# Hybrid attention and RWKV block: the recurrence written in six parts a step, the first norm kept in DRAM, pools handed over while the preparation ends

## The chip, the cores and the metric

The kernel runs on one core of a Trainium2 chip. The metric is the device time of one execution in microseconds. TensorE is PE in the profile, VectorE DVE, ScalarE ACT, GpSimd POOL and SyncE SP; SP issues all of the kernel's DMAs.

## What is computed

One layer of a hybrid backbone on 2048 latent tokens and 256 context tokens of width 1024, float32:

```python
h  = modulate(rmsnorm(x, norm1_g), shift1, scale1)       # hc: the same of the context
q, k, v, rw, gl = jnp.split(h @ w_in, IN_SPLITS, axis=-1)
ya = latent_window_attention(rope(q), rope(k), v, kc, vc, sink)   # 128-token blocks, |i-j| <= 128, and all context keys
# RWKV-7, both directions d, 8 heads of 64; each latent scan starts from that direction's context state
sa = jnp.einsum('bhvk,bhk->bhv', S, -kk_t)
S  = S * w_t[:, :, None, :] + sa[..., None] * b_t[:, :, None, :] + v_t[..., None] * k_t[:, :, None, :]
y  = jnp.einsum('bhvk,bhk->bhv', S, r_t)
yr = rwkv_output(y_d0 + y_d1, ...)                       # group norm, bonus, low-rank gate
ga, gr = jnp.split(jax.nn.sigmoid(gl), 2, axis=-1)
x = x + gate1 * ((ga * (ya @ w_branch_attn) + gr * (yr @ w_branch_rwkv)) @ w_out)
x = x + gate2 * (jnp.square(jax.nn.relu(h2 @ w_mlp_up)) @ w_mlp_down)   # h2: second norm, modulated
out = rmsnorm(x, norm_f_g)
```

## The kernel before

Large products are made of three float32r matmuls each: both operands are split into a high part (a rounding copy on ScalarE) and a low part (a subtraction, here on GpSimd), and high x high, high x low and low x high are summed in PSUM (`gemm`, L215 to L217).

*First norm and input projection.* Tokens are taken in three thirds of two blocks each: (0,256) and (256,512), then (1280,384) and (768,512), then (1664,384) and (2048,256), as (first token, count). `norm_block` loads and normalises a block (L180), transposes it on TensorE into `tr` (L186), modulates it on VectorE into `hf` (L188) and splits `hf` into `hh` (ScalarE, L192) and `hl` (GpSimd, L193). There is one pair of buffers for a third, so a third is split only when the third before it has been projected. `project` goes through 36 groups of 128 weight columns: 20 for queries, keys, values and RWKV inputs, 16 for the merge gates. For the first 1024 latents the gate groups are left for later: their `hf` goes to DRAM (`h_d`), and 32 gates (16 groups for each half of 512 tokens) are made beside the recurrence (`gate`, tile `gt`; 24 matmuls each, the weights `gw_raw` split in `load_gw`, L829 and L830).

*Preparation.* After each third, `prepare` works off windows of 256 tokens (2, 4 and 3 of them): short convolution, decays (`zz_ps`), key norms (`nb_ps`), bonus (`bon_ps`), cumulated decays, on VectorE, ScalarE and GpSimd with small matmuls. It leaves keys, values and factors in DRAM (`ka_d`, `bk_d`, `rho_d`, `v_d`).

*Recurrence.* Each direction goes through 36 steps of 64 tokens; four steps are a window. For a window, `gram` makes the 64 x 64 products of its chunks (L517, after loading `kg` and `bkg`), and `inverse` inverts the unit triangular matrices: transposes and 31 substitution steps of two operations on VectorE (L528 to L549), then the off-diagonal part on TensorE (`yp`, `zp`, L557 and L569). `before` loads a step's operands, transposes them (`tb`, L606) and makes its masked products (`gb`, L613, masked at L616 and L617). `chain` is the dependent part of one step of one direction: products with the state (L624, evicted to `g`, L626), times the inverse (L629, evicted half by ScalarE at L630, half by VectorE at L631), the new state (L636 and L639, scaled by decay at L642), the outputs (L650 and L654). The loop takes direction 0, then direction 1, of each step and calls the two next parts of the next window's grams and inverse after each.

*Beside it.* After every second step `beside` emits a whole attention block (`attention`: 16 score tiles `sc` with their minima on VectorE, L754, then `sT`, the exponentials and `ops`), three parts of the later adaLN rows (`adp`, L117) and three gates, and from the twelfth call on the attention branch's product with its weights (`branch`, L881 to L883, also in tile `gt`). 

*What sets the order.* The program is written in this order, and a scheduler decides at build time, from the order of writing, the dependences, the pools' buffers and estimated durations, which instruction stands where in each engine's queue. At run time each engine works off its queue in that order and waits on semaphores. Pools that close give their memory to those that open later. Behind the recurrence follow the merge (L990 on) and the MLP (`fu`, `fd`), which the change leaves as they are.

## Time and profile before

| what | us |
|---|---|
| median of three runs | 4351.41 |
| lowest, highest | 4349.32, 4365.3 |
| the profiled execution | 4355.38 |
| its span, first to last instruction | 4353.6 |

The program's stages in the trace, by the starts of TensorE's instructions: projections and preparations up to 997.2 us (last projection matmul), first chain matmul at 1134.3, last one's outputs at about 2410, two attention blocks until 2489, branches until 2537, merge until about 2950, MLP until 4353. A busy TensorE is read together with its granted clock, as a part of full speed: matmul times are modelled and overlap each other, so the same number of matmuls is busy for longer at a lower clock.

### The profile page before, as it was taken

How to read it: one execution, taken by the hardware profiler on the slowest of the kernel's cores; microseconds unless marked ns; L12 is line 12 of the kernel's file. 1: busy time of each engine (PE TensorE's matmuls, PEld its weight loads, DVE VectorE, ACT ScalarE, POOL GpSimd, SP SyncE). 2: the span in 40 equal slices, each digit the busy share in tenths (PEclk: the TensorE clock that was granted, in tenths of full speed). 3: DMA queues.
4: the chain of work that ended last, by engine and by line, in shares of the span. 5: the costliest groups of instructions: out<-in, count | busy, mean ns of one | idle time of the engine just before them, and what ended most of it. 6: DMA issues, size and time to landing. Idle time of an engine off the chain costs nothing.

```text
span 4353.6 us, 67896 instructions
## 1 busy us (share of the span) xinstructions
PE 3976.6 (91%) x26788; PEld 3218.5 (74%) x26788; DVE 2233.9 (51%) x3918; ACT 1305.1 (30%) x2332; POOL 1344.6 (31%) x1120
## 2 busy tenths in 40 slices
PE   7989969894899999989989768998999999999999
PEld 5868868793677777767767646777888888888887
DVE  2264286687556646656674245434444436443434
ACT  3353444553322322223222213332222123212121
POOL 3353554542111111001000046523433233433332
PEclk8979989895999999889989779999999999999999
DMA  6555556665444543354453145452211113221111
GB/s 216 143 183 155 160 159 190 175 200 177 140 116 123 165 128 112 112 144 147 120 160 110 45 133 186 161 172 75 83 54 58 39 55 120 73 63 50 48 49 49
DMA packets 581874, 527.84 MB, mean 121 GB/s; under 512 B 118452, under 2 KB 492948, under 8 KB 580532
## 3 DMA queue, kind: packets, MB, share of 16 engines
q1 hardware_dynamic: 581556, 523.50, 39.9%
q8 instruction: 211, 3.46, 0.3%
q14 instruction: 107, 0.88, 0.1%
HBM read 383.19 MB, written 140.18 MB: 120 GB/s over the span
## 4 chain that ended last, share of the span: by engine, by line
PE 59%; DVE 9%; DMA 4%; issue 2%; POOL 2%; ACT 1%; SPq 1%; POOLq 0%; DVEq 0%; ACTq 0%
PE fd L1185 5%; PE fd L1184 5%; PE fd L1186 5%; PE fu L215 5%; PE fu L216 5%; PE fu L217 5%; PE gb L613 2%; PE ops L788 2%; DVE st L545 1%; PE sc L744 1%; DVE itmp L534 1%; PE mm L1099 1%; PE mm L1100 1%; PE mm L1101 1%; DVE tn L536 1%
## 5 line engine op out<-in xcount | busy, mean ns | idle before, releaser
L215 PE MATMUL acc<-hh,w_hi 128*128 128x384 f32 (+6 forms) x1304 | 460.1, 355 | 24.6 <-DVE st L227 8.7
L216 PE MATMUL acc<-hl,w_hi 128*128 128x384 f32 (+6 forms) x1304 | 461.2, 354 | 10.9 <-POOL hl L193 7.2
L217 PE MATMUL acc<-hh,w_lo 128*128 128x384 f32 (+6 forms) x1304 | 456.7, 352 | 10.2 <-POOL w_lo L209 8.9
L1190 DVE TENSOR_TENSOR acc<-fd,acc 128x512 f32<-128x512 f32 x480 | 322.2, 686 | 249.5 <-PE fd L1186 247.7
L1174 DVE TENSOR_TENSOR g_l<-rl,g_h 128x512 fp32r<-128x512 f32 x128 | 161.7, 1265 | 486.4 <-POOL rl L1173 486.4
L215 PE MATMUL fu<-h2h,up_h 128*128 128x512 f32 x1024 | 403.3, 394 | 5.1 <-ACT rl L1171 5.1
L1184 PE MATMUL fd<-dn_h,g_h 128*128 128x512 f32 x1024 | 399.7, 390 | 4.9 <-DVE acc L1188 4.9
L216 PE MATMUL fu<-h2l,up_h 128*128 128x512 f32 x1024 | 402.7, 393 | 0.0
L217 PE MATMUL fu<-h2h,up_l 128*128 128x512 f32 x1024 | 401.9, 393 | 0.0
L1185 PE MATMUL fd<-dn_l,g_h 128*128 128x512 f32 x1024 | 399.9, 391 | 0.0
L1186 PE MATMUL fd<-dn_h,g_l 128*128 128x512 f32 x1024 | 398.3, 390 | 0.0
L209 POOL TENSOR_TENSOR w_lo<-w_raw,w_hi 128x1024 fp32r<-128x1024 f32 (+1 forms) x92 | 223.2, 2428 | 229.9 <-ACT w_hi L208 213.4
L215 PEld LDWEIGHTS acc<-hh,w_hi 128*128 128x128 f32 (+2 forms) x1304 | 258.4, 199 | 48.2 <-DVE st L227 6.6
L1173 POOL TENSOR_TENSOR rl<-rl 128x512 f32<-128x512 f32 x128 | 146.3, 1144 | 474.8 <-ACT g_h L1172 474.7
L216 PEld LDWEIGHTS acc<-hl,w_hi 128*128 128x128 f32 (+2 forms) x1304 | 259.1, 199 | 34.4 <-POOL hl L193 11.5
L217 PEld LDWEIGHTS acc<-hh,w_lo 128*128 128x128 f32 (+2 forms) x1304 | 257.5, 198 | 33.5 <-POOL w_lo L209 11.1
L1171 ACT ACTIVATE rl<-fu 128x512 f32<-128x512 f32 x128 | 76.2, 597 | 661.5 <-PE fu L217 654.3
L1128 POOL TENSOR_TENSOR dn_l<-raw,dn_h 128x1024 fp32r<-128x1024 f32 x64 | 155.6, 2448 | 275.7 <-ACT dn_h L1127 275.7
L830 POOL TENSOR_TENSOR gw_lo<-gw_raw,gw_hi 128x1024 fp32r<-128x1024 f32 x32 | 76.7, 2398 | 519.2 <-ACT gw_hi L829 440.6
L215 PEld LDWEIGHTS fu<-h2h,up_h 128*128 128x128 f32 x1024 | 192.9, 188 | 48.7 <-ACT rl L1171 5.8
L1184 PEld LDWEIGHTS fd<-dn_h,g_h 128*128 128x128 f32 x1024 | 192.8, 188 | 46.0 <-DVE acc L1188 5.3
L217 PEld LDWEIGHTS fu<-h2h,up_l 128*128 128x128 f32 x1024 | 192.8, 188 | 43.2
(295 smaller groups left out, 8580.1 us busy)
## 6 DMA issues: line engine op xcount, KB each, us to landing
w_raw<-in_w_in SPq DMA_DIRECT2D x74, 512.0 KB
raw<-in_w_mlp_up SPq DMA_DIRECT2D x64, 512.0 KB
raw<-in_w_mlp_down SPq DMA_DIRECT2D x64, 512.0 KB
bk_d<-bk SPq DMA_DIRECT2D x36, 512.0 KB
bkg<-bk_d SPq DMA_DIRECT2D x72, 256.0 KB
w<-v_d SPq DMA_DIRECT2D x144, 128.0 KB
gw_raw<-in_w_in SPq DMA_DIRECT2D x32, 512.0 KB
ada_w<-in_w_ada SPq DMA_DIRECT2D x32, 512.0 KB
```

The lines of the kernel that those rows point to most:

```text
L209: pool.tensor_tensor(out=lo[:, :, :m], in0=raw[:, :, :m], in1=hi[:, :, :m].bitcast(F32), op=ALU.subtract)
L215: pe.matmul(ps[:m, :n], wh[:, k, :m], hh[:, k, :], start=(k == 0), stop=False)
L216: pe.matmul(ps[:m, :n], wh[:, k, :m], hl[:, k, :], start=False, stop=False)
L217: pe.matmul(ps[:m, :n], wl[:, k, :m], hh[:, k, :], start=False, stop=(k == KC - 1))
L613: pe.matmul(gs[h][:, p], bk[r, p], s.kr[r, h:3:2 - h, p], start=True, stop=True)
L1128: eng.tensor_tensor(out=lo, in0=raw, in1=hi.bitcast(F32), op=ALU.subtract)
L1173: pool.tensor_tensor(out=rl, in0=rl, in1=rl, op=ALU.mult)
L1174: dve.tensor_tensor(out=glo[:, j], in0=rl, in1=gh[:, j].bitcast(F32), op=ALU.subtract)
L1184: pe.matmul(ps, lh, dn[j][0][:, cs], start=(j == 0), stop=False)
L1185: pe.matmul(ps, lh, dn[j][1][:, cs], start=False, stop=False)
L1186: pe.matmul(ps, ll, dn[j][0][:, cs], start=False, stop=(j == FG - 1))
L1190: dve.tensor_tensor(out=acc[:, cs], in0=ps, in1=acc[:, cs], op=ALU.add)
```

## The change

- `norm_block` is split. It now yields `hf`; `norm_store` writes the slices to `h_d`, which holds all tokens; `split_block` splits them. The blocks of the second and third thirds are normalised and stored during the first third's projection, one after every three groups; later they are loaded and split, with the low parts of even slices on VectorE, of odd ones on GpSimd.
- The projection's pools (`pg1`) close before the preparation's own. The pools of grams and inverse (`inv`), `auxp`, `gtp` and `gates` open before the last preparation has ended, on the other side of memory. Window 0's grams and 24 gate parts (a gate is now four parts of six matmuls, with its weights loaded a gate ahead) are emitted there; window 0's inverse goes forward beside attention and gates.
- A step has six parts for both directions together: products with the state, products with the inverse, state and outputs, transposes of the next step, and its masked products, one direction each. After each part one part of the next window is emitted, and `beside`, which advances attention, gate or branch, and attention again by one yield each. All recurrence matmuls are linked to their predecessor in the written order (`InOrder`).
- Operands of a step and of a gram are loaded one step ahead; `bkg` is half as large, in rows of 256 bytes in place of 512. `g` and all of `w` are evicted by ScalarE. The inverse is cut into finer parts. adaLN products draw on `auxp` in place of `atp`.
- Attention is two generators, `scores` and `outputs`; a block's outputs are emitted beside the next block's scores. Context keys stand in tiles of their own, latent keys in two sets for two blocks each.

```diff
+    prp = p1.enter_context(tc.tile_pool(name="prp", bufs=3, space=PSUM, side="right"))
+    pg1 = ExitStack()
...
+    def norm_store(t0, n):
+        for k, hf in norm_block(t0, n):
+            sp.dma_start(out=h_d[:, k, t0:t0 + n], in_=hf)
...
-            act.activation(hi[:, k, :], hf[:, :n], AF.Copy)
-            pool.tensor_tensor(out=lo[:, k, :], in0=hf[:, :n], in1=hi[:, k, :].bitcast(F32), op=ALU.subtract)
+        first = (t0, n) in THIRDS[0]
+        for k, hf in norm_block(t0, n) if first else load():
...
+            act.activation(hi[:, k, :], hf, AF.Copy)
+            (pool if first or k % 2 else dve).tensor_tensor(out=lo[:, k, :], in0=hf, in1=hi[:, k, :].bitcast(F32),
+                                                            op=ALU.subtract)
...
+            for j, b in enumerate(b for third in THIRDS[1:] for b in third):
+                project(THIRDS[i], hs, groups[3 * j:3 * j + 3])
+                norm_store(*b)
...
+        def link(self, r):
+            if self.last is not None:
+                tc.add_manual_dep(r.ins, self.last.name,
...
-        dve.tensor_copy(g, cp[:, 0])
+        act.activation(s.g, s.cp[:, 0], AF.Copy)
...
-        dve.tensor_copy(w[C:P, 0, 1], cp[C:P, 0])
+        act.activation(w[C:P, 0, 1], cp[C:P, 0], AF.Copy)
...
-            if k % 6 == 0:
+            if k % 3 == 0:
                 yield
...
-            ps = bank(atp, "adp", "at")
+            ps = bank(auxp, "adp", "aux")
...
-    p1.close()
+    pg1.close()
...
-    p1.close()
+    pg1.close()
...
+    first = window(0, sts)
+    for i in range(5):
+        next(first)
+    for _ in range(EARLY):
+        next(flr, None)
...
+    for i, _ in enumerate(first):
...
+        beside(1)
...
-            for d in range(2):
-                nxt = open_step(step + 1, d) if step + 1 < NCH else None
-                chain(sts[w], cur[d], nxt)
...
+            nxts = [open_step(step + 1, d) if step + 1 < NCH else None for d in range(2)]
+            for part in range(6):
+                if part == 0:
+                    for s in cur:
+                        chain_g(s)
+                    next(mods, None)
+                elif part == 1:
+                    for s in cur:
+                        chain_u(sts[w], s)
+                elif part == 2:
+                    chain_s(cur, nxts)
+                elif part == 3 and nxts[0] is not None:
+                    for s in nxts:
+                        turn(s)
+                elif part > 3 and nxts[0] is not None:
+                    before(nxts[part - 4])
+                next(ahead_of, None)
+                beside(TICKS)
```

What this does to TensorE's queue, at three places. First, before, the end of the last preparation: `zz_ps` and `bon_ps` are its last products, `sc` the first attention block's scores, `gt` the first gate.

```order
L413 MATMUL zz_ps<-xlr_8130,decay_w_r 128x256
L413 MATMUL zz_ps<-xlr_8136,iclr_a_r 128x256
L456 MATMUL bon_ps<-ks,c_1766 128x256 x2
L744 MATMUL sc_10392<-kA,qA 128x256
L746 MATMUL sc_10392<-kB,qB_9525 128x256
L744 MATMUL sc_10393<-kA,qA 128x256
L746 MATMUL sc_10393<-kB,qB_9525 128x256
L751 LDWEIGHTS idb_9513
L751 MATMUL sc_10392<-amask,idb_9513 128x128
L215 MATMUL gt<-gh,gw_hi 128x512
```

The same place after the change, at the last `zz_ps`.

```order
L947 MATMUL gt<-gl,gw_hi 128x512
L947 MATMUL gt<-gh,gw_lo 128x512
L433 MATMUL zz_ps<-xlr_8218,decay_w_r 128x256
L433 MATMUL zz_ps<-xlr_8224,iclr_a_r 128x256
L947 MATMUL gt<-gh,gw_hi 128x512
```

Gate matmuls stand ahead of, between and behind the preparation's last products: 72 ahead of the last `bon_ps` where there were none, 222 ahead of the first chain matmul where there were 54.

Second, the middle of the recurrence before: the two directions' chains (one `ch` number for each step of a direction) are at different points of their steps.

```order
L624 MATMUL ch_21038<-w,kr 64x64 x8
L882 MATMUL gt<-ya_l,wa_h 128x512
L883 MATMUL gt<-ya_h,wa_l 128x512
L636 MATMUL ch_20927<-w,ident 64x256 x2
L639 MATMUL ch_20927<-w,bt 64x64 x8
L629 MATMUL ch_21038<-g,st 64x64 x8
L650 MATMUL ch_20927<-bm,w 64x64 x8
L654 MATMUL ch_20927<-kr,w 64x64 x8
L613 MATMUL gb<-kr,bks 128x128 x8
```

A like place after the change; L535 is the line in `InOrder` that emits every recurrence matmul.

```order
L535 MATMUL ch_21944<-g,st 64x64 x8
L535 MATMUL g<-kg,bkg 64x64 x16
L535 MATMUL ch_21933<-w,ident 64x256 x2
L883 MATMUL ops<-vtok,pT 128x65 x4
L535 MATMUL ch_21944<-w,ident 64x256 x2
L535 MATMUL ch_21933<-w,bt 64x64 x8
L535 MATMUL ch_21944<-w,bt 64x64 x8
L835 MATMUL sc_22178<-kAl_9618,qA 128x384
L837 MATMUL sc_22178<-kBl_9620,qB_9627 128x384
```

Both directions are at the same point of the step now, and what stands between two of its blocks is a gram, attention or a gate.

Third, the end of the recurrence before: `ch_23990` is the last step of the direction that ends last.

```order
L650 MATMUL ch_23990<-bm,w 64x64 x8
L654 MATMUL ch_23990<-kr,w 64x64 x8
L744 MATMUL sc_22189<-kA,qA 128x256
L746 MATMUL sc_22189<-kB,qB_9525 128x256
L744 MATMUL sc_22198<-kA,qA 128x384
```

The same place after the change.

```order
L535 MATMUL ch_24111<-kr,w 64x64 x8
L535 MATMUL ch_24122<-kr,w 64x64 x8
L988 MATMUL gt<-ya_h,wa_h 128x512
L989 MATMUL gt<-ya_l,wa_h 128x512
L990 MATMUL gt<-ya_h,wa_l 128x512
```

Before, two attention blocks and 96 branch matmuls follow the last chain matmul; now 36 branch matmuls do.

## Rows read from the trace of the kernel before

**Rows 1.** the page: busy time of each engine, TensorE's clock in 40 slices

```profile
PE 3976.6 (91%) x26788; PEld 3218.5 (74%) x26788; DVE 2233.9 (51%) x3918; ACT 1305.1 (30%) x2332; POOL 1344.6 (31%) x1120
...
PEclk8979989895999999889989779999999999999999
```

**Rows 2.** windows by stage; columns: length, PE, PEld, DVE, ACT, POOL busy, clock, DMA

```profile
208.00:310.00 102.00, 83.04 (x338) 65.31 (x337) 70.48 (x125) 54.41 (x111) 62.06 (x71) 0.78 0.62 197
590.00:670.00 80.00, 55.12 (x269) 47.96 (x268) 65.28 (x132) 39.27 (x93) 41.20 (x52) 0.76 0.52 153
997.20:1134.30 137.10, 66.39 (x587) 49.76 (x586) 93.07 (x185) 44.15 (x90) 39.17 (x50) 0.61 0.51 153
1134.30:2410.00 1275.70, 1201.14 (x13544) 923.84 (x13543) 763.95 (x1634) 348.90 (x629) 118.64 (x83) 0.94 0.45 132
2410.00:2489.00 79.00, 67.49 (x344) 52.93 (x338) 24.81 (x62) 18.53 (x30) 0.20 (x1) 0.68 0.06 16
2489.00:2537.00 48.00, 29.79 (x97) 20.05 (x96) 4.82 (x7) 4.34 (x7) 7.49 (x6) 0.75 0.45 145
```

**Rows 3.** timeline of PE: start, duration, line, idle before and its releaser

```profile
1056.55 1.19 PE L456 MATMUL bon_ps<-ks,c 128*128 128x256 f32 x2 [17.16 <-DVE ks L453]
...
1078.37 0.58 PE L744 MATMUL sc<-kA,qA 128*128 128x256 f32 x1 [18.73 <-DVE qA L729]
```

**Rows 4.** groups of PE, 1134.3 to 2410: busy us, mean ns, idle before, releasers

```profile
L629 PE MATMUL ch<-g,st 64*64 64x64 f32 x1152 | 61.4, 229 | 4.0 <-DVE g L626 3.9
...
L650 PE MATMUL ch<-bm,w 128*64 128x64 f32 x1008 | 52.9, 238 | 7.6 <-DVE w L642 7.4
...
L744 PE MATMUL sc<-kA,qA 128*128 128x384 f32 x104 | 49.1, 473 | 10.5 <-DVE mm L754 9.8 <-DVE qA L729 0.3 <-ACT ob L800 0.3
L517 PE MATMUL g<-kg,bkg 64*64 64x64 f32 x1024 | 46.4, 226 | 11.1 <-DMA bkg<-bk_d 9.2 <-ACT ga L518 1.6
...
L557 PE MATMUL yp<-t,ga 32*32 32x32 f32 x1024 | 30.8, 218 | 10.0 <-DVE t L549 9.9
...
L117 PE MATMUL adp<-ada_w,silr 128*32 128x256 f32 x256 | 20.7, 394 | 10.6 <-DMA ada_w<-in_w_ada 10.6
```

**Rows 5.** windows: first third's projection, and the busiest projecting stretch of DMA

```profile
100.00:120.00 20.00, 20.00 (x112) 17.29 (x111) 1.94 (x4) 5.05 (x9) 5.05 (x6) 1.00 0.45 137
660.00:680.00 20.00, 16.67 (x104) 16.11 (x103) 14.89 (x34) 9.20 (x20) 7.14 (x6) 0.91 0.85 262
```

**Rows 6.** timeline of PE: two gate matmuls in a row

```profile
1136.51 0.39 PE L215 MATMUL gt<-gh,gw_hi 128*128 128x512 f32 x1
1136.73 0.39 PE L216 MATMUL gt<-gl,gw_hi 128*128 128x512 f32 x1
```

**Rows 7.** the page's groups: low halves of gate weights

```profile
L830 POOL TENSOR_TENSOR gw_lo<-gw_raw,gw_hi 128x1024 fp32r<-128x1024 f32 x32 | 76.7, 2398 | 519.2 <-ACT gw_hi L829 440.6
```

**Rows 8.** groups, whole run: the two evictions of w

```profile
L631 DVE COPY w<-ch 64x256 f32<-64x256 f32 x72 | 30.7, 427 | 31.1 <-ACT w L630 29.7
...
L630 ACT ACTIVATE w<-ch 64x256 f32<-64x256 f32 x72 | 26.8, 374 | 76.7 <-PE ch L629 66.0 <-DVE tn L536 6.9 <-DVE itmp L534 1.6
```

**Rows 9.** windows: 100 us of the recurrence

```profile
2300.00:2400.00 100.00, 98.44 (x1085) 76.09 (x1085) 46.46 (x109) 24.62 (x44) 0.30 (x2) 1.00 0.34 102
```

**Rows 10.** timeline of DVE, and of POOL beside it, at the first switch

```profile
280.14 0.73 DVE L180 TENSOR_SCALAR x<-x,ss_n 128x1024 f32<-128x1024 f32 x1
...
287.27 2.88 DVE L180 TENSOR_SCALAR x<-x,ss_n 128x1024 f32<-128x1024 f32 x1
290.07 2.46 DVE L437 TENSOR_SCALAR ta<-ta,kab,kaa 128x256 f32<-128x256 f32 x1
...
287.01 2.55 POOL L209 TENSOR_TENSOR w_lo<-w_raw,w_hi 128x1024 fp32r<-128x1024 f32 x1
...
289.56 2.82 POOL L209 TENSOR_TENSOR w_lo<-w_raw,w_hi 128x1024 fp32r<-128x1024 f32 x1
```

**Rows 11.** the page's groups: a VectorE subtraction of two SBUF operands

```profile
L1174 DVE TENSOR_TENSOR g_l<-rl,g_h 128x512 fp32r<-128x512 f32 x128 | 161.7, 1265 | 486.4 <-POOL rl L1173 486.4
```

More of the change, by code (lines that the diff above doesn't have):

```diff
@@ L612, in before @@
             for h, r in enumerate(hh):
-                pe.matmul(gs[h][:, p], bk[r, p], s.kr[r, h:3:2 - h, p], start=True, stop=True)
+                rpe.matmul(gs[h][:, p], s.bk[r, p], s.kr[r, h:3:2 - h, p], start=True, stop=True)
         for h in range(2):
@@ new lines, in chain_s @@
+    def chain_s(pair, nxts):
+        if nxts[0] is not None:
+            for s in pair:
+                for h, r in enumerate(hh):
+                    rpe.matmul(s.cp[r, 0], ident[r, r], s.w[r, 1, h], start=True, stop=False, skip_group_check=True)
+            for s, nxt in zip(pair, nxts):
+                for p in range(NP):
+                    for h, r in enumerate(hh):
+                        rpe.matmul(s.cp[r, 0, p], s.bt[:, p, r], s.w[:, 0, h, p], start=False, stop=True,
+                                  skip_group_check=True)
+                for h, r in enumerate(hh):
+                    dve.tensor_tensor(out=nxt.w[r, 1, h], in0=s.cp[r, 0],
+                                      in1=pc[r, s.d, :, s.c:s.c + 1].broadcast_to([C, NP, C]), op=ALU.mult)
+        if pair[0].step < NCC:
+            return
+        for s in pair:
@@ L647, in chain @@
-        with tc.issue_after(last.ins) if last is not None else ExitStack():
+                    rpe.matmul(s.cp[r, 1, p], s.w[:, 0, h, p], s.bm[:, h, p], start=(p == 0), stop=False,
+                              skip_group_check=True)
+        for s in pair:
             for p in range(NP):
                 for h, r in enumerate(hh):
-                    pe.matmul(yp[r, p], w[:, 0, h, p], s.bm[:, h, p], start=(p == 0), stop=False,
+                    rpe.matmul(s.cp[r, 1, p], s.w[r, 1, h, p], s.kr[r, 2, p], start=False, stop=True,
@@ L841, in load_h, with gate @@
         return hi, lo
-    def gate(t0, g, hi, lo):
-        wh, wl = load_gw(groups[20 + g][2])
+    def gate(g, hi, lo, t0, w):
         ps = bank(gtp, "gt", "gt")
-        gemm(ps, wh, wl, hi, lo, P, GBL)
+        for k in range(KC):
+            for x, y in ((w[0], hi), (w[0], lo), (w[1], hi)):
+                pe.matmul(ps, x[:, k], y[:, k], start=(k == 0 and x is w[0] and y is hi),
+                          stop=(k == KC - 1 and x is w[1]))
+            if k % 2 and k < KC - 1:
+                yield
         ob = gap.tile([P, GBL], F32, name="gob", bufs=2)
-        act.activation(ob, ps[:, :GBL], AF.Tanh, scale=0.5)
+        act.activation(ob, ps, AF.Tanh, scale=0.5)
         sp.dma_start(out=g_d[g, :, t0:t0 + GBL], in_=ob)
+        yield
     def branch_weights(brp, raw_of):
@@ L885, in branch, with attend @@
             sp.dma_start(out=ma_d[j, :, ts], in_=gt)
-    gate_work = [(t0, g) for t0 in range(0, GL8R, GBL) for g in range(16)]
-    sts = []
-    for _ in window(0, sts):
-        pass
+            yield
+    load_k(kAc, kBc, 0, CTX)
+    outs = 0
+    def attend():
+        nonlocal outs
+        prev = None
+        for n in range(NB + 1):
+            k = None
+            if n < NB:
+                k = Block()
+                k.n = n
+            a = scores(k) if k is not None else iter(())
+            b = outputs(prev) if prev is not None else iter(())
+            while True:
+                more = [next(b, b) is not b, next(a, a) is not a]
+                yield
+                more.append(next(b, b) is not b)
+                yield
+                if not any(more):
+                    break
+            outs = n
+            prev = k
@@ new lines, in fill, with raw_of @@
+    def fill():
+        work = [(t0, g) for t0 in range(0, GL8R, GBL) for g in range(16)]
+        nxt = load_gw(groups[20][2])
+        for i, (t0, g) in enumerate(work):
+            if g == 0:
+                h = load_h(t0)
+            w = nxt
+            if i + 1 < len(work):
+                nxt = load_gw(groups[20 + work[i + 1][1]][2])
+            yield from gate(g, *h, t0, w)
+        pg.close()
+        brp = p2.enter_context(tc.tile_pool(name="branch", bufs=1, reuse_waits="tile"))
+        def raw_of(shape):
+            return brp.tile(shape, F32, name="raw", tag="raw", bufs=2)
+        wa = branch_weights(brp, raw_of)
+        for t in range(SEQ // GBL):
+            while outs < (t + 1) * GBL // P:
+                yield
+            yield from branch(brp, raw_of, wa, t)
```

345 lines of the change are left out of this document (187 added, 158 removed).

## Prediction, written before the changed kernel had run

> **What bounds the kernel now.** First the page's head: TensorE is busy 91% of the span, and no other engine over 51% [rows 1], so TensorE is the engine to look at. But its clock row falls below full in many slices [rows 1], and a busy TensorE at 0.6 of its clock does 0.6 of the work. So the second view is the windows, one row for each stage of the program, with busy time and granted clock side by side. Busy time times clock is about the work at full clock; what is left of the stretch is lost, to idle time or to a low clock (1.2 instead of 2.4 GHz is 0.5 in these rows) [rows 2]:
>
> - two switches between thirds of the input projection: 102.0 - 83.04 x 0.78 = 37 us lost, and 80.0 - 55.12 x 0.76 = 38 us lost;
> - from the last projection matmul to the first chain matmul: 137.1 us for 66.39 x 0.61 = 40 us of work, 97 lost;
> - first to last chain matmul: 1275.7 us for 1201.14 x 0.94 = 1129 us of work, 147 lost (75 idle, 72 by the clock);
> - the two attention blocks and the branches that stand alone behind the chain: 127 us for 67.49 x 0.68 + 29.79 x 0.75 = 68 us of work, 59 lost.
>
> The last three are one stretch of 1540 us with 1238 us of work: 303 us lost. The timeline of TensorE names the two long gaps in the first of them: 17.16 us for the preparation's VectorE work, 18.73 us for the first queries [rows 3]. VectorE works 93.07 of those 137.1 us [rows 2]: the preparation's tail and then the first inverse, one after the other, so this stretch is VectorE's, and TensorE has nothing ready to do beside it. In the recurrence the groups of TensorE instructions show no single culprit: a gram's load 11.1 us, the adaLN weights 10.6, the scores' reductions 10.5, the inverse's transposes 10.0, the state product 7.6, the first eviction 4.0 [rows 4].
>
> **The change part by part.** The number of matmuls doesn't change, so TensorE's full-clock work stays where it is in total; only what it loses can change. I go by stage.
>
> *Norms in the first third.* The four later blocks are normalised while the first third is projected, and a switch then only loads a slice, copies it and subtracts. The first third is TensorE at 20.00 of 20 us at full clock, with VectorE at 1.94 and DMA at 0.45, 137 GB/s [rows 5]: the added VectorE, ScalarE and GpSimd work is hidden there by matmuls, the transposes on TensorE aren't (they move from one place to the other at the same cost). What must fit is traffic: 1536 tokens of 4 KB read and the same written, 12.6 MB, while twelve groups are projected: 12 x 24 matmuls of 512 columns at 0.23 us [rows 6] and as many of 256 columns at half of that, 99 us. That is 127 GB/s on top of 137, 264 in all; the busiest projecting stretch shows 262 GB/s at a share of 0.85 [rows 5]. It fits, barely; if it doesn't, weights come late and TensorE waits. At a switch some 12 us stay lost (the first load, copy and subtraction before anything can start, then slices that arrive no faster than one a microsecond or two, beside two or four windows of preparation). Of 75 us lost that gives back 50 at best (I take 45 as the end), nothing if the preparation itself holds the switch, and below nothing, -30, if the loads collide. I take 25, the middle of the positive side, since at 220 to 300 us VectorE is as full with preparation as with norms.
>
> *End of the preparation.* Before the first chain matmul there stand 222 gate matmuls now, 54 before (the order). A gate matmul takes 0.23 us from start to start at full clock [rows 6]: 168 x 0.23 = 39 us of work come forward, 79 us in all. The length of the stretch is VectorE's: 93 us, which don't get fewer, with the first grams now in the midst of it instead of at its end. I give it 114 us, between 95 (VectorE without a gap) and 137 (as before): 35 lost instead of 97. The new wait here: gate matmuls stand in TensorE's queue ahead of the last preparation matmuls, and wait for their weights' low halves from GpSimd, 2.4 us each [rows 7]. If those are late, VectorE, which needs the preparation's products, is late too, and with it the inverse and the first chain. That is a rival below.
>
> *Recurrence.* Work: 1129 - 39 (gates gone forward) + 60 (the attention and branch tail, now beside the steps; 68 less the 8 that stay) = 1150 us. Lost time, with three things moved. Grams are loaded a step ahead, which removes most of the 11.1 us; scores come one head at a time between other work, against the 10.5; both directions' products stand in blocks with attention, gate or gram matmuls between them, against 7.6 + 4.0, and the inverse ends earlier within its window, against 10.0 [rows 4]. That is 43 of 75 idle us; I let 25 go, since each cause is pressed and not removed. The clock's 72 us go with idle time about one to one in this stage [rows 2], so 25 of them, too. The evictions of g and of half of w go from VectorE to ScalarE: half of w takes 427 ns there and 374 on ScalarE [rows 8], and with g alike, 144 operations or some 60 us are moved from an engine busy 60% to one busy 27% [rows 2]; on the path each hand-over is as long as before, so I book nothing. The last five steps have no attention left beside them: four bare hand-overs each of about half a microsecond, 10 us. Lost: 147 - 50 + 10 = 107 us. The ends: the best 100 us of this stage, 98.44 busy at clock 1.00 [rows 9], lose 1.6 us, which over 1150 is 18; unchanged is 147.
>
> The written order has its price. All recurrence matmuls now follow each other in one written order, so one late operand (of an inverse's product, from VectorE) holds every later recurrence matmul of both directions; adaLN products now draw on the same two PSUM banks as the grams, masks and inverses. The 10.6 us wait for adaLN weights stays, and there it holds the recurrence.
>
> *Tail.* Behind the last chain matmul stand 36 branch matmuls, 8 us, instead of two attention blocks and 96: 12 us with a start-up of 4, instead of 127.
>
> *Sum.* Before 137 + 1276 + 127 = 1540 us. After 114 + (1150 + 107) + 12 = 1383. Gain 157, with 25 from the norms 182. The profiled execution took 4355.4 us (span 4353.6 and 1.8 around it), which is 4 us over the median of the runs, so 4173 on its scale and about 4170 on theirs.
>
> **A rule against the split.** When GpSimd subtracts from two SBUF operands, VectorE instructions beside it stretch: one of 0.73 us took 2.88 us, and one of the preparation 2.46 us, under two GpSimd subtractions of 2.55 and 2.82 us [rows 10]. The change puts every other low half at a switch on VectorE, with two SBUF operands, the other on GpSimd. A VectorE subtraction of 512 columns with both operands in SBUF takes 1.265 us in the MLP, where GpSimd works too [rows 11]; 16 of them that exclude GpSimd instead of running beside it are 20 us over the two switches. The norms then bring 5 and not 25. The Trainium skill, "SBUF — State Buffer", Who interferes with whom, says that a VectorE instruction with two SBUF inputs and a GpSimd one that reads SBUF exclude each other for the whole instruction. By that rule the time is the 4193 below; the stretched rows show such waiting for VectorE instructions with one tensor operand, and no row shows it for two.
>
> **The rivals.**
> - *Slower.* The chain becomes a row of bare waits: both directions now reach each hand-over together, so neither covers the other, as it did before. Price: with S us lost in the recurrence the gain is 303 - 35 - 4 - S + 25 = 289 - S. It turns to a loss beyond 289, 8 us a step over 36 steps; at 10 us a step, S = 360 and the time is 4426. Against it: the order shows 2 to 10 us of other matmuls between dependent blocks in nearly all steps, and the operation between them is 0.4 us [rows 8]. For it: queues fixed by an estimate, and one late operand stops all.
> - *The recurrence gains nothing.* Inverses and adaLN products hold the single row, and S = 180, over today's 147: gain 289 - 180 = 109, time 4246.
> - *The end of the preparation gains nothing.* Gate matmuls hold it up: lost 97 plus 15 there; gain 182 - 77 = 105, time 4250.
> - *The norms' traffic collides with the weights.* -30 in place of 25: 4228.
> - *VectorE and GpSimd exclude each other at the switches.* 4193, as worked out above.
> - *Everything dense.* S = 40 and 45 from the norms: gain 289 + 20 - 40 = 269, time 4086.
>
> **How the numbers follow.** Forecast (4140 to 4190) 0.41; exclusion 0.10; traffic 0.08; preparation 0.12; recurrence as before 0.10; dense 0.10; slower 0.05; and 0.04 for two of the middle ones together, most of which comes to no change. The likeliest gives 4170. The range leaves out the slower case and part of the dense and the doubled ones: 4085 to 4290. Half a per cent, 22 us, is about what can be told from no change: faster 0.91, same 0.03, slower 0.06.
>
> **What would show it.** In the windows: the stretch from the last projection matmul to the first chain matmul at 105 to 125 us with clock above 0.7 (rival: 140 or more, gate matmuls waiting for GpSimd's low halves in it). The recurrence at some 1257 us, a little under the 1276 of before though it holds 21 us more work; its idle time under 50 us, without a gram's load or reductions among the large waits. Behind the last chain matmul the branch's end within 15 us. The switches with TensorE's lost time near 25 each, and VectorE's subtractions either 0.7 us (beside GpSimd) or above 1.2 us (excluded). The prediction is wrong if chain matmuls wait over 5 us a step on ScalarE or VectorE, if the first third's matmuls wait for weights, or if the merge behind the recurrence starts late and gives back what its beginning gained.

## The result

The changed kernel takes 4223.62 us (median of four runs, 4212.27 to 4228.56) against 4357.48 us before (four runs): a ratio of 0.9689, 95% interval 0.9659 to 0.9719, 134 us faster. The prediction was 4170 us, 4085 to 4290. The profiled execution took 4228.56 us, with a span of 4226.8.

The page of the changed kernel, TensorE's busy time and its clock in 40 slices, to be read against [rows 1]: the share is the same 91%, and the clock is no better.

```profile
PE 3865.3 (91%) x26788; PEld 3148.4 (74%) x26788; DVE 2171.9 (51%) x3794; ACT 1359.5 (32%) x2476; POOL 1349.6 (32%) x1104
...
PEclk8999979897999989797897889999999999999999
```

The windows of the stages, as in [rows 2] (length, busy time of PE, PEld, DVE, ACT, POOL, then clock and DMA). The first three go by the marks of the prediction: last projection matmul, first and last chain matmul, end of the branches. The last three take the middle marks at the first and the last new state, since the first chain matmul is only a first product that needs no inverse.

```profile
976.50:1124.30 147.80, 108.39 (x736) 79.91 (x735) 104.61 (x194) 54.93 (x105) 57.97 (x56) 0.76 0.64 179
1124.30:2400.80 1276.50, 1147.42 (x13805) 901.42 (x13801) 717.09 (x1559) 418.01 (x802) 108.16 (x83) 0.90 0.44 126
2400.80:2419.00 18.20, 11.29 (x40) 8.53 (x39) 4.43 (x9) 1.26 (x2) 2.06 (x2) 0.81 0.62 182
976.50:1136.30 159.80, 120.39 (x893) 88.51 (x892) 109.47 (x206) 61.24 (x119) 59.79 (x57) 0.78 0.64 182
1136.30:2376.00 1239.70, 1110.62 (x13372) 873.57 (x13373) 705.13 (x1531) 406.94 (x778) 103.32 (x78) 0.90 0.43 125
2376.00:2419.00 43.00, 36.09 (x320) 27.79 (x315) 11.53 (x26) 6.02 (x13) 5.07 (x4) 0.92 0.57 173
```

The same second set of marks for the kernel before:

```profile
997.20:1150.10 152.90, 82.19 (x734) 62.40 (x735) 97.88 (x199) 48.94 (x98) 39.17 (x50) 0.65 0.49 144
1150.10:2387.90 1237.80, 1163.24 (x13174) 893.70 (x13175) 752.78 (x1605) 335.98 (x608) 118.64 (x83) 0.94 0.46 134
2387.90:2537.00 149.10, 119.38 (x659) 90.48 (x658) 35.98 (x85) 30.99 (x50) 7.69 (x7) 0.75 0.19 61
```

Put side by side, in the two profiled executions:

| stage | before, us | after, us | difference |
|---|---|---|---|
| span's start to the last projection matmul | 997.2 | 976.5 | -20.7 |
| to the first new state | 152.9 | 159.8 | +6.9 |
| first to last new state | 1237.8 | 1239.7 | +1.9 |
| last new state to the branches' end | 149.1 | 43.0 | -106.1 |
| merge and MLP | 1816.6 | 1807.8 | -8.8 |

Most of the gain stands in one line: the tail, 106 of 127 us. The steps themselves take as long as before, though the two attention blocks and most of the branch that stood bare behind them are beside them now. (The mark of 2410 us for the kernel before is 3 us early: its last chain matmuls end at 2413, so the tail was 124 us and not 127.) The 9 us of merge and MLP were not examined. And the total of TensorE's idle time from the last projection matmul to the branches' end is the same: 1540 - 1365 = 175 us before, 1442.5 - 1267.1 = 175 us after. What fell is TensorE's busy time, by 98 us, with the same matmuls. By groups, the masked products `gb` lost 33 us (143.6 to 110.3), the chain's six groups together 57, the attention's outputs `ops` 22 (groups overlap, so these don't add up to 98).

### The profile page after: what moved, and what is told of

Its sections match the earlier page's. It is cut to its first block, busy times and chain, and to the rows that moved or that the text cites. A ratio compares the mean times of both kernels' runs of the same rounds, so it can differ in the third digit from the quotient of the medians.

```text
span 4226.8 us, 67796 instructions
## 1 busy us (share of the span) xinstructions
PE 3865.3 (91%) x26788; PEld 3148.4 (74%) x26788; DVE 2171.9 (51%) x3794; ACT 1359.5 (32%) x2476; POOL 1349.6 (32%) x1104
## 4 chain that ended last, share of the span: by engine, by line
PE 58%; DVE 6%; DMA 4%; issue 2%; POOL 2%; SPq 1%; ACT 1%; POOLq 0%; DVEq 0%; ACTq 0%
PE fd L1343 5%; PE fd L1344 5%; PE fd L1345 5%; PE fu L235 5%; PE fu L236 5%; PE fu L237 5%; PE ch L535 5%; PE gt L947 3%; PE ops L883 3%; PE gb L535 2%; DVE au L582 1%; PE sc L835 1%; PE mm L1260 1%; PE mm L1258 1%; PE mm L1259 1%
## 5 line engine op out<-in xcount | busy, mean ns | idle before, releaser
L1333 DVE TENSOR_TENSOR g_l<-rl,g_h 128x512 fp32r<-128x512 f32 x128 | 150.0, 1173 | 487.4 <-POOL rl L1332 487.4
L229 POOL TENSOR_TENSOR w_lo<-w_raw,w_hi 128x1024 fp32r<-128x1024 f32 (+1 forms) x92 | 232.7, 2532 | 205.9 <-ACT w_hi L228 185.7
L845 DVE TENSOR_REDUCE mm<-sc 128x1 f32<-128x256 f32 (+1 forms) x256 | 119.0, 477 | 237.9 <-PE sc L837 152.2
```

The costliest lines, as they stand in the source:

```text
L229: pool.tensor_tensor(out=lo[:, :, :m], in0=raw[:, :, :m], in1=hi[:, :, :m].bitcast(F32), op=ALU.subtract)
L1333: dve.tensor_tensor(out=glo[:, j], in0=rl, in1=gh[:, j].bitcast(F32), op=ALU.subtract)
```

## The experiments

After the kernels' first comparison two theories stood. *Theory 1*: matmuls have become cheaper. *Theory 2*: the order of the queue loses less time. Later ones are named in the expectations. Ratios are against the kernel before, run beside on the same chip; microseconds are medians of at least four runs.

**Are the masked products cheaper, and does that shorten anything?** In the trace of before, a block of eight masked products often stood as four and four, first one row half, then the other; the links of the change keep the halves alternating. TensorE's timeline, before (a float32 matmul leaves two records, so x8 is four matmuls):

```profile
1129.80 1.16 PE L613 MATMUL gb<-kr,bks 64*128 64x128 f32 x8
...
1132.14 1.16 PE L613 MATMUL gb<-kr,bks 64*128 64x128 f32 x8
```

and after, all eight in the time of four:

```profile
1226.68 1.16 PE L535 MATMUL gb<-kr,bks 64*128 64x128 f32 x16
```

So e1 sets the halves apart in the changed kernel, and e2 links them in the kernel before.

```diff
-        for p in range(NP):
-            for h, r in enumerate(hh):
+        for h, r in enumerate(hh):
+            for p in range(NP):
                 rpe.matmul(gs[h][:, p], s.bk[r, p], s.kr[r, h:3:2 - h, p], start=True, stop=True)
```

> The changed kernel with one edit: in the masked products gb of a step, the four of the upper row half are written before the four of the lower, where the changed kernel alternates them. Number and size of matmuls are the same. Theory 1 (the change's gain in the recurrence comes from cheaper blocks: matmuls of the two row halves run side by side when they alternate): a block of four of one half took 1.085 us in the trace of before, a block of eight alternating ones 1.09 us in that of after, so 72 steps of a direction cost up to 72 x 1.08 = 78 us more, 4265 to 4305 us, with the busy time of PE up by as much. Theory 2 (the gain is less lost time from the order of the queue, a matmul costs what it cost): within 10 us of the changed kernel, 4215 to 4235.

Measured: 4220.13 us, ratio 0.9687 (0.9651 to 0.9724): no change. The group of masked products between the first and the last state, after (busy, mean ns, idle before and who ended it):

```profile
L535 PE MATMUL gb<-kr,bks 64*128 64x128 f32 x1088 | 103.1, 309 | 15.7 <-issue 8.4 <-DVE bm L678 5.5 <-PE sc L842 0.8
```

and in e1, with the stage's window below:

```profile
L535 PE MATMUL gb<-kr,bks 64*128 64x128 f32 x1088 | 135.7, 303 | 6.4 <-ACT bt L665 5.1 <-PE sc L837 0.6 <-issue 0.4
```

```profile
1139.20:2383.90 1244.70, 1141.62 (x13371) 907.40 (x13373) 709.70 (x1531) 405.55 (x778) 103.73 (x78) 0.90 0.43 124
```

The blocks are busy 33 us longer, and the stage is 5 us longer (1244.7 against 1239.7): nearly all of it came out of waiting.

```diff
+        last = None
         for p in range(NP):
             for h, r in enumerate(hh):
-                pe.matmul(gs[h][:, p], bk[r, p], s.kr[r, h:3:2 - h, p], start=True, stop=True)
+                m = nc.tensor.matmul(gs[h][:, p], bk[r, p], s.kr[r, h:3:2 - h, p], start=True, stop=True)
+                if last is not None:
+                    tc.add_manual_dep(m.ins, last.name,
+                                      mybir.DependencyInfo(mybir.DependencyClass.NoSync, mybir.DependencyReason.DATA))
+                last = m.ins
```

> The kernel before with one edit: the eight matmuls of each gb block are linked in their written order, so that the halves alternate; the scheduler may no longer put the four of one half first. Theory 1: some 33 of 72 blocks stood in two parts in the trace of before, 33 x 1.08 = 36 us, so the time falls by 20 to 40 us to 4318 to 4338. Theory 2: no change, within 10 us of 4357.

Measured: 4366.91 us, ratio 1.003 (1.0005 to 1.0056): if anything 0.3% slower, although the edit did its work: from the last projection matmul to the branches' end the masked products were busy for 123.9 us in place of 143.6. For the masked products, theory 1 falls in both directions; the other blocks, which are the larger part of the 98 us, were not tried alone. A block that is busy for a shorter time gains nothing where the next thing in the queue waits for another engine anyway; and with the halves apart, VectorE can mask the first while TensorE makes the second (both reasons are argued, not shown).

**Is it the written order?** e3 cuts all links; everything else of the change stays.

```diff
-            if self.last is not None:
+            if False:
                 tc.add_manual_dep(r.ins, self.last.name,
```

> The changed kernel without the links that keep the recurrence's matmuls in written order; the scheduler places them as before the change. Theory 1: halves of gb stand apart again (61 blocks of four in the order) and other blocks fall into pieces, which costs 33 to 60 us: 4255 to 4285. Theory 2, with its rival that one late operand in the single row holds all later matmuls: freeing the order gives lost time back, 4180 to 4215. Idle time of PE should fall in either; the busy time rises only by theory 1.

Measured: 4193.38 us (4191.14 to 4198.62), ratio 0.9624 (0.9592 to 0.9656). The links cost some 29 us; this kernel is faster than both. Its windows, from the last projection matmul to the first state, to the last state, and to the branches' end:

```profile
975.00:1138.00 163.00, 123.82 (x890) 91.95 (x888) 110.66 (x206) 61.01 (x118) 60.04 (x57) 0.76 0.64 178
1138.00:2352.70 1214.70, 1160.60 (x13403) 900.17 (x13402) 712.38 (x1533) 407.15 (x779) 102.31 (x77) 0.94 0.44 127
2352.70:2398.20 45.50, 38.29 (x301) 29.11 (x301) 17.05 (x35) 7.33 (x14) 14.70 (x15) 0.96 0.70 201
```

The waits of TensorE between the first and the last state (us in total, times, longest), with links:

```profile
PE sT L873 <- DVE mm L845: 26.3, 11, 5.9
PE sc L835 <- DVE qA L815: 11.9, 3, 6.1
PE ch L535 <- ACT w L695: 11.5, 8, 6.3
PE ch L535 <- DVE kr L676: 9.8, 3, 5.6
PE ch L535 <- DVE w L710: 9.6, 4, 8.3
PE ot L896 <- DVE on L890: 8.5, 4, 6.6
```

and without:

```profile
PE sT L873 <- DVE mm L845: 7.9, 4, 3.5
PE ch L535 <- DVE kr L676: 7.0, 5, 2.4
...
PE ch L535 <- DVE w L710: 5.0, 6, 1.7
...
PE ch L535 <- ACT w L695: 2.9, 3, 1.7
```

The idle time of this stage is 1239.7 - 1110.6 = 129 us with links and 1214.7 - 1160.6 = 54 us without, and each wait of the list is smaller. In the kernel before it was 1237.8 - 1163.2 = 75 us: without the links the change does lower the idle time, with them it raises it. The busy time is 50 us longer without, most of it in the masked products (103.1 to 139.4 us) and the chain's groups, and the stage still ends sooner: here too a shorter busy time was no gain.

e10 keeps the links inside a block and cuts them between blocks, by a line like this at the head of each kind of block:

```diff
+        rpe.last = None
```

> The changed kernel with its links kept inside a block (a gram, a transpose block, gb, the products with the state, and so on) and cut between blocks. With all links 4222 us, without any 4193. If the loss of 29 us comes from one row in which a late block holds all later ones, it is gone here: 4180 to 4200. If it comes from what holds a block together (halves of gb side by side give VectorE its first half later), it stays: 4210 to 4225.

Measured: 4215.02 us, ratio 0.9681 (0.9659 to 0.9703). Most of the loss stays, so it isn't the long row alone. The idle time between the first and the last state is 1231.1 - 1131.4 = 100 us, between the 129 and the 54. How much of the rest is the blocks and how much the sorting of the queues, which every edit does anew, stays open.

**Was it the norms?** e4 puts the first norm back to where it was.

```diff
-        first = (t0, n) in THIRDS[0]
-        for k, hf in norm_block(t0, n) if first else load():
-            if first and t0 >= CTX:
+        for k, hf in norm_block(t0, n):
+            if CTX <= t0 < CTX + GL8R:
...
-            for j, b in enumerate(b for third in THIRDS[1:] for b in third):
-                project(THIRDS[i], hs, groups[3 * j:3 * j + 3])
-                norm_store(*b)
-            project(THIRDS[i], hs, groups[12:20])
+            project(THIRDS[i], hs, groups[:20])
```

> The changed kernel with the first norm as it was: later blocks are normalised and split at the switches, low halves all on GpSimd, and only the first 1024 latents' slices are stored. The stage up to the last projection matmul was 20.7 us shorter after the change (976.5 against 997.2 us). If the norm edit brought that, the time rises by 15 to 25 us, to 4239 to 4249, with the last projection matmul near 997; if pools or weights did, it stays near 4224.

Measured: 4232.03 us, ratio 0.9712 (0.9678 to 0.9746), some 10 us over the change, with overlapping intervals. The last projection matmul starts at 991.8 us, 15 us later than after the change: most of that stage's gain is the norms', but part of it is given back behind. In e2 and e9, which keep the first norm of the kernel before, this matmul starts at 989.7 and 990.0 us, in the profiled execution of before at 997.2; so the stage's gain is 13 to 21 us.

**Was it the tail?** e5 takes the kernel without links and slows attention down, so that two blocks and the last branch stand bare behind the chain again.

```diff
-    TICKS, EARLY = 1.0, 24
+    TICKS, EARLY = 0.8, 24
```

> The changed kernel without the links (4193 us), and attention advanced at 0.8 of the pace: some two attention blocks and 96 branch matmuls stand behind the last chain matmul again, as before the change. Theory 3 (what the change gained lies mainly in covering that tail; the recurrence is as long as what stands in it plus its waits): the recurrence shortens by the 45 to 60 us of work moved out, the tail grows from 26 to 115 to 125 us, 4225 to 4255 in all. Rival (the recurrence took 1276 to 1290 us in all of the kernels so far, whatever stood in it, so something of its own sets its length): it stays near 1280, the tail adds all of its 90 us, 4275 to 4290. If the tail had nothing to do with it, no change.

Measured: 4230.28 us, ratio 0.9712 (0.9682 to 0.9741): 37 us slower than e3. Its windows from the first to the last chain matmul, and from there to the branches' end:

```profile
1090.70:2326.50 1235.80, 1154.87 (x13703) 908.89 (x13755) 707.85 (x1521) 403.56 (x775) 111.31 (x81) 0.92 0.46 130
2326.50:2456.50 130.00, 102.22 (x477) 77.86 (x483) 39.93 (x87) 33.75 (x55) 29.18 (x26) 0.79 0.32 89
```

The recurrence is 44 us shorter than in e3 (1280.1 by these marks) and the tail 104 us longer (25.8): the work that moved out shortens the steps, as theory 3 has it, and what stood bare lost 37 us more than it did beside them, by the medians. (The two windows give 60; some 14 of that come back behind the branches in these executions, which was not examined.)

**Is it the fine mixing?** e6, without the links like e3, writes the pieces that stood between the parts of a step at its end.

```diff
                 next(ahead_of, None)
-                beside(TICKS)
+            for part in range(6):
+                beside(TICKS)
             cur = nxts
```

> The changed kernel without the links (4193 us), with the pieces of attention and gates that stood after each of a step's six parts written all at the step's end. Theory 4 (the fine mixing of six parts a step gains): 20 to 60 us slower, 4213 to 4250, with more idle time at chain matmuls. Rival (where the scheduler may place them, the place in the writing counts for little; what counts is that attention goes forward evenly): within 10 us of 4193.

Measured: 4212.09 us (4196.79 to 4218.91), ratio 0.9661 (0.9629 to 0.9693). The interval overlaps that of e3, so this doesn't tell them apart: 0 to 20 us.

e8, also without the links, writes a block's outputs behind its scores; it was meant to keep the pace.

```diff
-            a = scores(k) if k is not None else iter(())
-            b = outputs(prev) if prev is not None else iter(())
+            def both():
+                yield from scores(k)
+                yield from outputs(k)
```

> The changed kernel without the links (4193 us), with a block's outputs written behind its own scores instead of beside the next block's, at the same pace. In the changed kernel the transposed scores sT wait 26 us for reductions on VectorE that free the two PSUM banks they share with the scores; without the links 8 us. If that sharing is a cost of the mixing, time falls by 5 to 15 us; if the mixing covers the softmax between the two halves of a block, it rises by 10 to 40 us.

Measured: 4240.68 us, ratio 0.9736 (0.9702 to 0.977), 47 us slower than e3. So mixing two blocks isn't the cost that the shared PSUM banks made it look like. How much it gains stays open, since the pace changed as well: attention ended at 2285 us here, 136 us before the last chain matmul, in e3 at 2334 us, 38 us before it.

**Do the evictions matter?** The prediction booked nothing for them. Three kernels ask it: e7 (without links) and e12 (with links) give the two copies back to VectorE, e9 moves them to ScalarE in the kernel before.

```diff
-        act.activation(s.g, s.cp[:, 0], AF.Copy)
+        dve.tensor_copy(s.g, s.cp[:, 0])
...
-        act.activation(w[C:P, 0, 1], cp[C:P, 0], AF.Copy)
+        dve.tensor_copy(w[C:P, 0, 1], cp[C:P, 0])
```

> The changed kernel without the links (4193 us), with g and the second half of w evicted by VectorE, as before the change. The prediction booked nothing for this: within 10 us of 4193. If the two halves of w one after the other on ScalarE cost on the path (0.4 us a step and direction), the time falls by up to 72 x 0.4 = 29 us; if VectorE's inverse holds up evictions, it rises by up to as much.

Measured: 4238.44 us, ratio 0.9728 (0.9695 to 0.976), 45 us slower than e3. The waits of TensorE between the first and last state:

```profile
PE sT L873 <- DVE mm L845: 22.7, 12, 5.5
PE ch L535 <- DVE kr L676: 10.5, 4, 5.7
...
PE ch L535 <- DVE w L695: 7.9, 7, 1.9
...
PE ch L535 <- DVE g L687: 3.4, 3, 1.5
```

Against e3's list above, the wait for g and w is 7.9 + 3.4 where it was 2.9, and the largest growth is elsewhere: the transposed scores wait 22.7 us in place of 7.9 for reductions, which stand in the same queue of VectorE as the copies.

```diff
-        dve.tensor_copy(g, cp[:, 0])
+        act.activation(g, cp[:, 0], AF.Copy)
...
-        dve.tensor_copy(w[C:P, 0, 1], cp[C:P, 0])
+        act.activation(w[C:P, 0, 1], cp[C:P, 0], AF.Copy)
```

> The kernel before with one edit, taken from the change: g and the second half of w are evicted by ScalarE instead of VectorE. Giving these back to VectorE cost the changed kernel without links 45 us (4238 against 4193). Theory 5 (VectorE's queue, with the inverse in it, holds up what the chain waits for, before as well as after): 20 to 45 us faster than before, 4312 to 4337. Rival (in the order of before the other direction's work covers these evictions, and it is the two directions in step that uncovered them): within 10 us of 4357.

Measured: 4333.17 us against 4355.47, ratio 0.9953 (0.993 to 0.9977). One part of the change alone is worth 20 us. Between the first and the last state the idle time of TensorE falls from 75 to 1221.7 - 1163.4 = 58 us at the same busy time, and the waits of the chain for g and w, 3.9 and 4.3 us before, are gone from the list.

> The changed kernel, links and all, with g and the second half of w evicted by VectorE again: the one part of the change undone in the changed kernel itself (4222 us). The prediction booked nothing for it. Undone without the links it cost 45 us, done in the kernel before it gave 22 us; any edit also makes the scheduler sort the queues anew, and e6 and e11 showed 19 and 24 us for edits that should have been worth little. If the part is worth what it was in the other two, 4244 to 4267; if those were the scheduler's doing, 4210 to 4235.

The edit is that of e7. Measured: 4244.18 us, ratio 0.9723 (0.9688 to 0.9758), against 0.9689 for the change: 15 us by the ratios, with overlapping intervals. All three have the same sign; 15 to 45 us. The wait of the transposed scores doesn't follow, though: 26.3 us after the change, 20.0 here. So which of VectorE's later operations paid is shown for none of the three.

**Would less work on VectorE give more?** e11, without the links, moves 16 subtractions of the queries' low half to GpSimd.

```diff
-        dve.tensor_tensor(out=qA[C:P], in0=qraw[C:P], in1=qA[C:P].bitcast(F32), op=ALU.subtract)
+        pool.tensor_tensor(out=qA[C:P], in0=qraw[C:P], in1=qA[C:P].bitcast(F32), op=ALU.subtract)
```

> The changed kernel without the links (4193 us), with the low half of the queries (16 subtractions of 64 x 1024, 1.2 us each on VectorE) made by GpSimd, which is busy 9% of the recurrence. If VectorE's queue is what holds the recurrence, 20 us less in it give 5 to 20 us: 4173 to 4188. Rival (GpSimd is slower at it and, while it reads, stretches VectorE's inverse, as the stretched rows at the first switch showed for other instructions): 0 to 15 us slower, 4193 to 4208.

Measured: 4216.96 us (4200.36 to 4225.32), ratio 0.9675 (0.9644 to 0.9706): not faster than e3's 0.9624, and likely slower. Taking 20 us off VectorE isn't a gain by itself. Between the first and the last state a subtraction took 2.36 us on GpSimd, 1.22 on VectorE in e3, and the inverse's two substitution operations grew by 5 us in all. Whether these or the new sorting of the queues made the difference, was not tried.

## Why the prediction was right, and where it was wrong

The direction and the range held; the forecast was 54 us too low. By its own terms, on the profiled execution: the sum gave 4173 us, and 4173 + 34 (end of the preparation) + 19 (recurrence) + 6 (tail) + 4 (norms) - 9 (merge and MLP, not predicted) = 4227. That it came so near is in part luck: the recurrence is only 19 us off because two errors of over 100 us each cancel in it (below).

*Tail: right.* 12 us forecast, 18.2 measured by the same marks. The extra is waits for the branch's sums on VectorE (6.9 us, 5.67 the longest). By the marks this term is most of the gain, but its work went into the recurrence, so the marks say where the time went and not what saved it. e5 shows that covering it was worth 37 us net in the kernel without links. The rest of the gain lies in what let the recurrence take that work in without growing: the evictions (15 to 45 us), perhaps the mixing of blocks (e8), less the links. No run adds these up in the changed kernel.

*End of the preparation: the step that failed most.* 114 us forecast, 147.8 measured; and by the first new state nothing was gained at all (152.9 before, 159.8 after). The forecast took VectorE's busy time and some idle time as the length, and had no term for what TensorE does after the first inverse has left VectorE. The last transposes of that inverse, before and after:

```profile
1111.85 2.49 DVE L549 STREAM_TRANSPOSE t<-st 32x1024 f32<-32x1024 f32 x2
```

```profile
1094.15 1.24 DVE L603 STREAM_TRANSPOSE t<-st 32x1024 f32<-32x1024 f32 x1
```

They end 117.1 us after the last projection matmul before and 118.9 us after: VectorE's part is 5 us over the 114, and no shorter than it was. The other 29 of the 34 us lie between that end and the first chain matmul (20 us before). The next product, `yp`, needs these transposes; it started 3.7 us behind them before and 11.5 us behind them after:

```profile
1118.07 0.31 PE L557 MATMUL yp<-t,ga 32*32 32x32 f32 x4
```

```profile
1106.86 0.25 PE L535 MATMUL yp<-t,ga 32*32 32x32 f32 x4
```

In TensorE's timeline 24 gate matmuls, a block of masked products and the first scores stand in these 11.5 us, and from the inverse's end to the first new state TensorE is busy nearly throughout, before and after:

```profile
1114.40:1150.10 35.70, 35.70 (x491) 29.21 (x491) 8.68 (x23) 15.15 (x26) 2.50 (x2) 1.00 0.25 68
```

```profile
1095.40:1136.30 40.90, 39.37 (x516) 30.28 (x516) 17.08 (x36) 16.96 (x29) 9.61 (x5) 0.93 0.66 175
```

So gate matmuls that were brought forward stood in front of the chain's own products. That is half of the rival for this stage: its sign, 140 us or more, was there, but the gates' waits for GpSimd's low halves are not among TensorE's large waits.

VectorE's own part didn't shrink either. Up to the first chain matmul its busy time rose from 93.07 to 104.61 us (11 operations `x<-u,pp,x` of the preparation, 5 us, fall into the stretch now; others ran longer), and its idle time stayed, 44.0 and 43.2 us. The largest single piece of it comes from a gate again. ScalarE's timeline after the change (start, duration, line, idle before and its releaser):

```profile
994.96 0.47 ACT L437 ACTIVATE ta<-zz_ps,ha 128x256 f32<-128x256 f32 x1
1005.28 0.63 ACT L938 ACTIVATE gh<-graw 128x512 fp32r<-128x512 f32 x1 [9.85 <-DMA graw<-h_d]
1005.82 0.46 ACT L435 ACTIVATE lam<-zz_ps,hw 128x256 f32<-128x256 f32 x1
1006.17 0.46 ACT L437 ACTIVATE ta<-zz_ps,ha 128x256 f32<-128x256 f32 x1
```

A slice of the gates' input, `gh`, stands in ScalarE's queue ahead of the preparation's own `lam` and `ta`, and waits 9.85 us for its load. VectorE's timeline shows who paid:

```profile
995.80 0.68 DVE L440 TENSOR_TENSOR_SCAN cum<-c,lam 128x256 f32<-128x256 f32 x1
1006.67 0.88 DVE L451 SCALAR_TENSOR_TENSOR bk<-ta,kk 128x256 f32<-128x256 f32 x1 [10.19 <-ACT ta L437]
```

These are 10.19 us without work on VectorE. But VectorE waited for the same `ta` before, too: 8.7 us in three places, the longest 5.9; it is 11.7 us in two places now. The prediction asked what stands behind the new matmuls on TensorE and who waits for GpSimd; it didn't ask what stands behind their loads' copies on ScalarE, nor what the gates hold up behind the inverse. No run took either out alone, so their shares of the 34 us are read from the trace, not shown by an experiment.

*Recurrence: work did not stay, lost time did not fall.* Forecast: 1150 us of work and 107 lost, 1257. Measured: 1276.5, with 1147.4 busy at clock 0.90. Busy time times clock is 1033 by that, 117 us less than the work that should have been there, and what that leaves as lost is 243 us, 136 more than forecast; the two cancel but for 19. The idle time rose from 75 to 129 us, where a fall to 50 was forecast. The failed step is the first one, "busy time times clock is about the work at full clock". Written in larger blocks, with both row halves alternating, the same matmuls are busy for a shorter time, without the program being shorter: e1 added 33 us of busy time to the masked products and 5 us to the stage. So "lost" was not a store to draw on: in e1 the waits took up nearly all that the blocks saved. The rise of the idle time is the links': without them (e3) it is 54 us between the first and the last state, against 75 before, about the fall that was forecast.

*The written order* was called a price and put at nothing in the sum; e3 puts it at 29 us of time and 75 us of idle time. The rival that named it (one row held by its latest operand, S = 180) would have the recurrence at 1330 us and was too high; and by e10 the long row isn't all of the 29.

*The evictions* were booked at nothing, since ScalarE's copy takes as long as VectorE's and hand-overs stay. They were worth 15 to 45 us (e7, e9, e12), more than the copies' own difference of some 0.05 us each. The likely reason is the queue they stood in, VectorE's, in which the inverse and the scores' reductions stand too; the waits that shrank are not the same ones in the three pairs, so this is argued and not shown.

*Norms: right in size.* 25 us forecast, 20.7 measured up to the last projection matmul, 15 of it the norm edit's and about 10 of it left at the end (e4). The traffic fitted: between 37 and 200 us the DMAs moved 192 GB/s where it was 142 (264 was forecast for the first third), and TensorE's list of waits names no DMA. The rival by the rule on VectorE and GpSimd gave 4193 and 5 us from the norms; the stage shows 20.7. The group of VectorE's low halves, 512 columns, and GpSimd's:

```profile
L212 DVE TENSOR_TENSOR hl<-hf,hh 128x512 fp32r<-128x512 f32 x4 | 3.5, 865 | 10.9 <-ACT hh L211 10.9
```

```profile
L212 POOL TENSOR_TENSOR hl<-hf,hh 128x512 fp32r<-128x512 f32 x12 | 15.4, 1284 | 24.5 <-ACT hh L211 24.5
```

The mean of 0.865 us, between the 0.7 and the 1.2 us that the prediction named for the two cases, is a mixture. Two of the four took 0.69 us; the other two began well inside a subtraction of GpSimd's and ended half a microsecond behind it, like this one:

```profile
252.08 1.29 POOL L212 TENSOR_TENSOR hl<-hf,hh 128x512 fp32r<-128x512 f32 x1 [2.72 <-ACT hh L211]
```

```profile
252.70 1.22 DVE L212 TENSOR_TENSOR hl<-hf,hh 128x512 fp32r<-128x512 f32 x1 [6.13 <-ACT hh L211]
```

Nine of the sixteen VectorE subtractions at the switches began while GpSimd was subtracting. Seven of them ended 0.41 to 0.59 us behind GpSimd's end; beside the other two, which took their usual 0.55 us, GpSimd's took longer (1.52 us in place of 1.0, 4.53 in place of 2.4). The rule of the Trainium skill, "SBUF — State Buffer", Who interferes with whom, speaks for exclusion of two such instructions, and these pairs agree with it. What was wrong in the rival is the price: it took all sixteen to exclude GpSimd, 20 us; together they were busy for 12.6 us, some 4 more than sixteen undisturbed ones (0.69, 0.55 and 0.41 us for 512, 384 and 256 columns).

*The slower case* didn't come: the three waits of chain matmuls in the list above are 11.5 + 9.8 + 9.6 = 31 us over 36 steps, under 1 us a step where the loss began at 8.

## What to carry to other kernels

A bare stretch behind a chain is a safe gain to look for, but its length isn't its price: the work moves into the chain, and of 104 us of tail 37 were won by covering it (e5). Don't add up "lost time" from busy time and clock as if a cheaper block or a removed wait were paid out in full; ask for each saved microsecond what the engine waits for next. When work is brought forward or moved, go through every engine's queue that it passes, the copies behind its loads and the products that it now stands in front of too, and when an operation changes engines, price the queue it leaves, not its duration alone.

## What was not expected of the hardware

Eight float32 matmuls of 64 rows, with the two row halves alternating, took 1.16 us, as did four of one half, all at a granted clock of 1.00 (the two timelines above): the halves ran side by side. It shortened the busy time by 33 us between the first and the last state, and the kernel by nothing (e1; e2 the other way round, by 20).

Edits that should be worth a few microseconds moved the time by about 20 (e6, e11). The scheduler sorts every queue anew with each edit, which may be the reason; no run shows it, and the interval of e6 overlaps that of e3. Until that is known, a single edit of less than about 0.5% is weak evidence in a kernel like this.
